# Unread matrix products in the doubling, ahead of the sparse attention's transposes and of block 1's output product

## The chip, the cores and the metric

The kernel runs on one core of a Trainium2 chip. Five engines work beside each other and wait for one another through semaphores: TensorE (PE in the profile; its weight loads are PEld), VectorE (DVE), ScalarE (ACT), GpSimd (POOL) and SyncE (SP), which issues most transfers. [...] The metric is the time of one execution on the device in microseconds, the median of several runs.

## The reference

The reference puts two blocks of two layers each behind one another, on 256 tokens of width 1024. A layer of block 1 mixes three attention branches and ends with one output product. A layer of block 2 runs three mixers side by side (gated linear attention, RWKV-7, sparse attention), an output product, a norm and a feed-forward part. What the change stands next to is this:

```python
# block 1, end of a layer
merged = jnp.sum(gates * up, axis=2)
return x + jnp.einsum('bsd,de->bse', merged, w_out)

# block 2, RWKV-7: one step per token
def step(state, inp):
    r_t, w_t, k_t, v_t, a_t, b_t = inp
    sa = jnp.einsum('bhvk,bhk->bhv', state, a_t)
    state = (state * w_t[:, :, None, :] + sa[..., None] * b_t[:, :, None, :]
             + v_t[..., None] * k_t[:, :, None, :])
    return state, jnp.einsum('bhvk,bhk->bhv', state, r_t)

# block 2, sparse attention: selected keys, and a window
pr = jax.nn.softmax(s, axis=-1)
return jnp.einsum('bghqnk,bgqnkd->bqghd', pr.astype(vg.dtype), vg)
```

With 256 tokens the selection and the window both hold all keys up to the query, so the kernel computes two causal attentions.

## The kernel before

**Tiling.** The tokens are two tiles of 128, the heads 64 wide. Weights come as a stream of pieces of 128x1024 through SyncE's queue (`unit`, L294); ScalarE rounds each to fp32r (`whi`, L295) and VectorE takes the rest (`wlo`, L272). Three products (L329 to L331 in `mm3`) then give an almost exact fp32 result; plain fp32 products go by L327.

**The doubling** (`rwkv`, L792). The steps of a 128-token tile are written as a triangular system. Its inverse is built by doubling in five levels, `q` from 1 to 5, for both tiles and four heads at once. A level has two rounds of sixteen 64x64 products: the first (L931) multiplies `M` with `Pm` into a pair of PSUM banks, and VectorE multiplies the pair with a mask (`r_X`, called at L933); the second (L951) multiplies `Qm` with `X`, VectorE adds the old `Pm` (`r_P`, L953), TensorE transposes it (L407) and ScalarE copies it out (`r_Q`, L908). The last level's second round (L959, L960) has another form. Each round uses columns 0 to 255 of its two banks. The bank pair comes from a pool that holds one pair, so the steps of a level follow each other. In the gaps the program has other work of the layer: products of the gated linear attention (L1120), of the compressed attention (L1216, L1247, L1289, L1309) and of RWKV itself (L888, L942).

**The sparse attention** (`nsa_direct`, L1258, through `causal_attn`, L534, and `softmax_pv`, L513). For each token tile and each of two key sets it goes in groups of up to four heads: scores (L547), the causal mask as one bf16 product of constants (`negb`, `causb`, L550), maximum (L518), scaling (L520), exponentials (L524), four transposes into one bank (`transposed`, L403, L407), a copy (L528) and the products with the values (L531). That is two groups for the first tile and four for the second, twelve in a layer. Scores, transposes and the attention's output take their banks from a pool of three, which other helpers share (`ps`, L248).

**Block 1's output product** (`out_proj`, L376, called by `block1_layer`, L652). Its left operand is split by ScalarE (`mh`, L400) and VectorE (`ml`, L275), and its weights come in four units; both must be there before the first products.

**Order.** The program is written as a list, and a planner orders it when the kernel is built: each instruction gets a running number, and among those that are ready in the planner's model the lowest goes first. `with self.sec(name)` (L204) shifts the numbers of a section by an entry of the table `AHEAD` (L1532). Each engine then runs its list in order. A PSUM buffer of a pool is taken when its first writer is placed and comes free behind its last reader.

Of the kernel before, what the change touches and what calls it, by code (L numbers as in the profile page):

```python
# [151 lines left out]
class Kern:  # L152
# [95 lines left out]
    def ps(self, *shape):  # L248
        return self.bank(self.pa, *shape)
# [123 lines left out]
        for p in range(2):  # L373
            done(p, ps[p])

    def out_proj(self, tags, parts, ps, ws, first=0, n=None, skew=0):  # L376


        n = n or len(tags)

        def go(i, tt, cg):
            h, lo = parts[i]
            sl = slice(128 * tt, 128 * tt + 128)
            for kk in range(2):
                self.mm3(ps[tt][cg], (h[:, kk, sl], lo[:, kk, sl]), w[i](1024 * kk + 512 * cg, 512),
                         first + i + kk == 0, first + i == n - 1 and kk == 1)
        w = [ws[i] if i in ws else self.unit(t) for i, t in enumerate(tags)]
        m = len(tags) - skew
        for i, tt, cg in ([(i, tt, cg) for i in range(m) for tt in range(2) for cg in range(2)] +
                          [(i, tt, cg) for tt in range(2) for cg in range(2) for i in range(m, len(tags))]):  # L390
            go(i, tt, cg)
# [8 lines left out]
            nc.scalar.activation(h, src, AF.Copy, scale=scale)  # L400
            self.stt(l, src, scale, h.bitcast(F32), ALU.mult, ALU.subtract)

    def transposed(self, ps, srcs):  # L403

        pt = ps(4, 128)
        for j, s in enumerate(srcs):
            self.nc.tensor.transpose(pt[:, j], s, self.ident)  # L407
        return pt[:, :len(srcs)]
# [14 lines left out]
    def rms(self, xs, g, xT, ps=None, out=None):  # L423

        nc = self.nc
        for tt in range(2):
            x = xs[tt]
            ss = self.sm.tile([128, 2], F32, name="ss")
            o = out[tt] if out is not None else self.u("xn", D)
            for cg in range(2):  # L430
                cs = slice(512 * cg, 512 * cg + 512)
                if ps is not None:
                    self.tt_(x[:, cs], ps[tt][cg], x[:, cs], ALU.add)
                nc.scalar.activation(xT.space(cg)[:, :, 128 * tt:128 * tt + 128], x[:, cs].rearrange("p (c s) -> p c s", c=4), AF.Square,
                                     accum_out=ss[:, cg:cg + 1])
            ms = self.sm.tile([128, 2], F32, name="ms")
            self.tt_(ms[:, 0:1], ss[:, 0:1], ss[:, 1:2], ALU.add)
            nc.vector.tensor_scalar(ms[:, 1:2], ms[:, 0:1], 1.0 / D, 1e-6, op0=ALU.mult, op1=ALU.add)
            rs = self.sm.tile([128, 1], F32, name="rs")
            nc.gpsimd.tensor_tensor(out=rs, in0=ms[:, 1:2], in1=self.mhalf[:, 0:1], op=ALU.pow)  # L440
            for cg in range(2):
                cs = slice(512 * cg, 512 * cg + 512)
                self.stt(o[:, cs], x[:, cs], rs, g[cg], ALU.mult, ALU.mult)
                if xT is not None:
                    xT.put(o[:, cs], cg, tt)

    def deep_norm(self, x, ps, w, b, xT=None, out=None, pool=None):

        nc = self.nc
        for tt in range(2):  # L450
            t = [self.u("dn") for cg in range(2)]
            st = self.sm.tile([128, 2, 6], F32, name="dn_s")
            for cg in range(2):
                cs = slice(512 * cg, 512 * cg + 512)
                self.stt(t[cg], x[tt][:, cs], ALPHA, ps[tt][cg], ALU.mult, ALU.add)
                nc.vector.bn_stats(out=st[:, cg], in_=t[cg])
            mv = self.sm.tile([128, 4], F32, name="dn_m")
            nc.vector.bn_aggr(out=mv[:, 0:2], in_=st.rearrange("p a b -> p (a b)"))
            nc.vector.tensor_scalar(mv[:, 2:3], mv[:, 1:2], 1e-5, None, op0=ALU.add)
            nc.gpsimd.tensor_tensor(out=mv[:, 3:4], in0=mv[:, 2:3], in1=self.mhalf[:, 0:1], op=ALU.pow)  # L460
            for cg in range(2):
                self.stt(t[cg], t[cg], mv[:, 0:1], w[cg], ALU.subtract, ALU.mult)
            for cg in range(2):
                cs = slice(512 * cg, 512 * cg + 512)
                self.stt(x[tt][:, cs], t[cg], mv[:, 3:4], b[cg], ALU.mult, ALU.add)
                if xT is not None:
                    xT.put(x[tt][:, cs], cg, tt, ps=pool)
                if out is not None:
                    nc.sync.dma_start(out[0, 128 * tt:128 * tt + 128, cs], x[tt][:, cs])

# [39 lines left out]
        self.nc.scalar.activation(t, ps, AF.Tanh, scale=0.5)  # L510
        self.stt(dst, t, 1.0, ps, ALU.add, ALU.mult)

    def softmax_pv(self, sv, heads, nk, scale, vt, o, ocol, den, first, last):  # L513

        nc = self.nc
        nh = len(heads)
# [6 lines left out]
        for i, h in enumerate(heads):  # L523
            nc.scalar.activation(p3[:, i], sv[:, i], AF.Exp, bias=nb[:, i:i + 1], scale=scale,  # L524
                                 accum_out=den[:, h:h + 1])
        pt = self.transposed(self.ps, [p[:, 128 * j:128 * j + 128] for j in range(nh * nk)])
        ps = self.u("ptsb", 4, 128)
        nc.scalar.copy(ps, pt)  # L528
        for i, h in enumerate(heads):
# [1 line left out]
                nc.tensor.matmul(o[:, ocol(h)], ps[:, i * nk + k, :], vt(k, h),  # L531
                                 start=first and i == 0 and k == 0, stop=last and i == nh - 1 and k == nk - 1)

    def causal_attn(self, qT, kT, v, tt, o, den, mask=None):  # L534

        nc = self.nc
        nk = tt + 1
# [5 lines left out]
        for gi, heads in enumerate(groups):  # L543
# [8 lines left out]
            else:  # L552
                nc.tensor.matmul(s3, self.negb, mask[:, None, :].to_broadcast([128, hs, 128 * nk]), start=False, stop=True)
            self.softmax_pv(s3, heads, nk, 0.125, v, o, lambda h: slice(64 * h, 64 * h + 64), den,
                            gi == 0, gi == len(groups) - 1)

    def gate_out(self, o, den, g2, nh, ysT, tt):

# [93 lines left out]
    def block1_layer(self, l, hT, mem):  # L652
# [70 lines left out]
        with self.sec("hw"):  # L723
            held = {1: self.unit(f"wo{l}.1", tag="vg")}
        with self.sec("wo"):
            self.out_proj([f"wo{l}.{u}" for u in range(4)], parts, ps, held, skew=3)
        return ps


# [62 lines left out]
    def rwkv(self, l, R, wa, g0, tl, P, hp, rows, out):  # L792
# [84 lines left out]
        half = (lo, up)  # L877
        tiles = [(tt, c) for tt in both for c in range(2)]
        quads = [(n, j, b) for n in range(4) for j in both for b in both]
        pair = lambda: self.pair(self.pr)[:, :, 0:256].rearrange("p a (n k) -> p a n k", n=4)  # L880
        eye = cst["eye64"]

        def products(tt, nm, st, pool):
# [11 lines left out]

        Pm = self.u("r_P", 4, 2, 64)
        nc.gpsimd.tensor_copy(Pm, eye[:, None, None].to_broadcast([128, 4, 2, 64]))
        ps = pair()
        for n, j, b in quads:
            tt, c = tiles[n]  # L900
            mm(ps[half[b], j, n], ar4[tt][half[j], 0, c, half[b]], Bt[half[j], c, 128 * tt + 64 * b:128 * tt + 64 * b + 64],
# [23 lines left out]
        rest = list(both)  # L925
        rhs, yv = [], self.c3("r_yv")
        for q in range(1, 6):
            ps = pair()
            for n, j, b in quads:
                tt, c = tiles[n]  # L930
                mm(ps[half[j], b, n], M[tt]["MB", j][half[b], c, 0, half[b]], Pm[half[b], n, j], start=n == 0, stop=n == 3)  # L931
            X = self.u("r_X", 2, 4, 64)
            self.tt_(X, ps, self.minv[:, 64 * q - 64:64 * q][:, None, None].to_broadcast([128, 2, 4, 64]), ALU.mult)  # L933
            if rest:
# [10 lines left out]
                nc.scalar.copy(yv[:, t0], ps[:, 1].rearrange("p h d -> p (h d)"))  # L945
                if t0:
                    nc.gpsimd.tensor_copy(rhs[t0][:, :, 64:128], TM[t0][:, 1].rearrange("p (h d) -> p h d", d=64))
            ps = pair()
            if q < 5:
                for n, j, b in quads:  # L950
                    mm(ps[half[b], j, n], Qm[half[j], n, b], X[half[j], b, n], start=n == 0, stop=n == 3)  # L951
                Pn = self.u("r_P", 4, 2, 64)
                self.tt_(Pn.rearrange("p n j k -> p j n k"), ps, Pm.rearrange("p n j k -> p j n k"), ALU.add)  # L953
                Pm = Pn
# [303 lines left out]
    def nsa_direct(self, qT, kT, vt, gc, out):  # L1258
# [3 lines left out]
        for tt in range(2):  # L1262
# [4 lines left out]
            for i, n in enumerate("sw"):  # L1267
                o = self.ps()
                self.causal_attn(qT[tt], lambda pr, h, m: kT[n][pr, :m], lambda k, h: vt[n][k][:, 64 * (h % 2):64 * (h % 2) + 64],
                                 tt, o, den[:, i])  # L1270
                nc.vector.reciprocal(cf[:, i], den[:, i])
                self.tt_(cf[:, i], cf[:, i], gate[:, 1 + i], ALU.mult)
                t = acc if i == 0 else self.u("n_t")
                self.tt_(h3(t), h3(o), cf[:, i, :, None].to_broadcast([128, 8, 64]), ALU.mult)
                if i:
                    self.tt_(acc, acc, t, ALU.add)
# [145 lines left out]
    def run(self, out, stop=None):  # L1422
        nc = self.nc
        with self.block(BUFS1):
            mem = self.mem_kv(0, nc.sync)
            self.load_first()
            kv = mem()
# [38 lines left out]
class Feat:  # L1466
# [5 lines left out]
        self.h = [kern.u(name + "h", 4, 256, dt=F32R) for _ in range(n // 4)]  # L1472
        self.l = [kern.u(name + "l", 4, 256, dt=F32R) for _ in range(n // 4)]

    def put(self, src, g, tt, scale=1.0, ps=None):

        pt = self.k.transposed(ps or self.k.ps, [src[:, 128 * j:128 * j + 128] for j in range(4)])
        sl = slice(128 * tt, 128 * tt + 128)
        self.k.split(pt, self.h[g][:, :, sl], self.l[g][:, :, sl], scale)

# [26 lines left out]
class Both(Feat):  # L1507
# [3 lines left out]
        super().__init__(kern, n, name)  # L1511
        self.w = Whole(kern, n, name)

    def put(self, src, g, tt, scale=1.0, ps=None):
        pt = self.k.transposed(ps or self.k.ps, [src[:, 128 * j:128 * j + 128] for j in range(4)])
        sl = slice(128 * tt, 128 * tt + 128)
        self.k.split(pt, self.h[g][:, :, sl], self.l[g][:, :, sl], scale)
        self.k.nc.scalar.copy(self.w.f[g][:, :, sl], pt)
# [11 lines left out]
         "r_g2 r_y r_RW r_yn r_ynx r_ynq dsh f_h f_l f_t oh ol",  # L1530
}.items() for n in names.split()}
AHEAD = dict(x=-107, x2=172, m01=267, n12=1422, h1=368, n3=-94, rwkv=38, cmp=242, w=-330, cpd=-15, h2=179, ww=-425, out=-24, gla=-582, ofg=488, ln2=-168, atta=-78, gin=-106, tok=36, imask=-432, rx1=-342, attb=-197, rxf=517, w1=15, feat=5, nsa=-131, ofn=-323, rx0=25, hw=499, ofr=-116, hd=-14, rin=10, prep=298, wo=-87, ln1=298)  # L1532
ALPHA = float((2 * DEPTH) ** 0.25)
SMALL = ["x", "mem", "norm_g", "mem_norm_g", "final_g", "ln1_w_2", "ln1_b_2", "ln2_w_2", "ln2_b_2"]
P_MU, P_W0, P_A0, P_V0, P_KK, P_KA, P_BA, P_RK, P_POSK, P_POSV, P_W2K, P_W2V, P_WA, P_G2, P_TAIL = (
# [69 lines left out]
```

## Time and profile before

| | |
|---|---|
| time, median of 3 runs | 1604.45 us (1598.08 to 1605.7) |
| the profiled execution's own time | 1608.67 us |
| its span, first to last instruction | 1606.6 us |
| mean granted clock of TensorE | 0.958 |
| busy: PE, PEld | 1543.5 us (96%), 1319.0 us (82%) |
| busy: DVE, ACT, POOL | 918.8 us (57%), 721.0 us (45%), 42.8 us (3%) |

Times of instructions are counted from the start of the span. A busy PE is not PE at its peak: products overlap, and their ends are modelled, so the distance from one start to the next tells what one costs. [...] Idle time stands before the instruction that ended it, with what it waited for.

### The profile page before, as it was taken

To read this page: it belongs to the slowest core of one execution; us is meant where nothing else is said; L and a number is where in the kernel's file an instruction comes from. 1 tells how busy PE (TensorE), PEld (TensorE's weight loads), DVE (VectorE), ACT (ScalarE), POOL (GpSimd) and SP (SyncE) were. 2 spreads that over 40 slices of the span, in tenths; PEclk is the share of its full clock that TensorE was granted. 3 is DMA by queue.
4 is the path that set the end of the run, shared out by engine and by line. 5 is a ranking of instruction groups with operands and counts; after the bars stand their busy time and mean duration, and the time that the engine had idled before them with its cause. 6 is when DMAs were issued, how large, how long until landed. Compare 5 with 4: busy or idle time off the path is not lost.

```text
span 1606.6 us, 25450 instructions
## 1 busy us (share of the span) xinstructions
PE 1543.5 (96%) x10196; PEld 1319.0 (82%) x10196; DVE 918.8 (57%) x1511; ACT 721.0 (45%) x1302; POOL 42.8 (3%) x82
## 2 busy tenths in 40 slices
PE   7999999999999999999999989999999999999997
PEld 6877899979878899868767769998797577789986
DVE  5566455565585455564445675556745455765554
ACT  5555544445454544454632234444355422344441
POOL 0000000000000000000001010000000000100000
PEclk9999999999999999999986899999999976999999
DMA  8643435455524345556301245557445111265560
GB/s 272 226 129 132 157 106 168 161 172 192 187 99 158 106 131 183 160 187 197 116 27 53 71 136 179 185 168 238 134 157 167 40 54 41 66 197 194 187 210 27
DMA packets 72982, 231.66 MB, mean 144 GB/s; under 512 B 8736, under 2 KB 11552, under 8 KB 72864
## 3 DMA queue, kind: packets, MB, share of 16 engines
q1 hardware_dynamic: 67248, 219.74, 41.5%
q10 hardware_dynamic: 5616, 10.30, 2.0%
q8 instruction: 80, 1.31, 0.3%
q14 instruction: 38, 0.31, 0.1%
HBM read 228.96 MB, written 1.05 MB: 143 GB/s over the span
## 4 chain that ended last, share of the span: by engine, by line
PE 44%; DVE 4%; ACT 3%; DMA 3%; issue 2%; POOL 0%; ACTq 0%; DVEq 0%
PE ps L329 9%; PE ps L331 9%; PE ps L330 9%; PE ps L327 3%; PE ps L407 3%; DMA raw<-in_stream_dram 2%; PE ps L1120 2%; PE ps L547 1%; PE ps L531 1%; DVE wlo L272 1%; PE ps L942 1%; ACT whi L295 1%; PE ps L888 1%; PE ps L931 1%; DVE xlo L272 0%
## 5 line engine op out<-in xcount | busy, mean ns | idle before, releaser
L272 DVE TENSOR_TENSOR wlo<-raw,whi 128x1024 fp32r<-128x1024 f32 (+2 forms) x364 | 427.8, 1184 | 324.3 <-ACT whi L295 321.3
L295 ACT CAST whi<-raw 128x1024 fp32r<-128x1024 f32 (+2 forms) x364 | 367.3, 1018 | 385.5 <-PE ps L330 165.4
L329 PE MATMUL ps<-xTh,whi 128*128 128x256 f32 x720 | 205.4, 285 | 5.2 <-ACT whi L295 4.0
L331 PE MATMUL ps<-xTh,wlo 128*128 128x256 f32 x720 | 205.1, 285 | 1.5 <-DVE wlo L272 1.5
L330 PE MATMUL ps<-xTl,whi 128*128 128x256 f32 x720 | 204.7, 284 | 0.0
L329 PEld LDWEIGHTS ps<-xTh,whi 128*128 128x128 f32 x720 | 138.5, 192 | 6.8 <-ACT whi L295 4.4
L331 PEld LDWEIGHTS ps<-xTh,wlo 128*128 128x128 f32 x720 | 138.6, 193 | 2.1 <-DVE wlo L272 2.1
L330 PEld LDWEIGHTS ps<-xTl,whi 128*128 128x128 f32 x720 | 138.5, 192 | 0.8
L330 PE MATMUL ps<-wlo,hTh 128*128 128x512 f32 (+2 forms) x352 | 135.8, 386 | 0.8 <-DVE wlo L272 0.8
L329 PE MATMUL ps<-whi,hTh 128*128 128x512 f32 (+2 forms) x352 | 134.9, 385 | 0.3 <-ACT wi L667 0.3
L331 PE MATMUL ps<-whi,hTl 128*128 128x512 f32 (+2 forms) x352 | 132.9, 378 | 0.0
L329 PE MATMUL ps<-hTh,whi 128*128 128x256 f32 x448 | 128.9, 288 | 0.0
L330 PE MATMUL ps<-hTl,whi 128*128 128x256 f32 x448 | 128.5, 287 | 0.0
L331 PE MATMUL ps<-hTh,wlo 128*128 128x256 f32 x448 | 127.6, 285 | 0.0
L524 ACT ACTIVATE pexp<-ps,nb 128x256 f32<-128x256 f32 (+1 forms) x144 | 60.0, 425 | 65.6 <-DVE nb L520 60.3
L329 PEld LDWEIGHTS ps<-hTh,whi 128*128 128x128 f32 x448 | 85.8, 192 | 0.8
L330 PEld LDWEIGHTS ps<-hTl,whi 128*128 128x128 f32 x448 | 85.7, 191 | 0.7
L331 PEld LDWEIGHTS ps<-hTh,wlo 128*128 128x128 f32 x448 | 85.7, 191 | 0.5
L329 PEld LDWEIGHTS ps<-whi,hTh 128*128 128x128 f32 x352 | 66.2, 188 | 13.9 <-issue 2.0
L330 PEld LDWEIGHTS ps<-wlo,hTh 128*128 128x128 f32 x352 | 66.3, 188 | 10.7 <-DVE wlo L272 1.2
L331 PEld LDWEIGHTS ps<-whi,hTl 128*128 128x128 f32 x352 | 66.2, 188 | 10.6
L518 DVE TENSOR_REDUCE mx<-ps 128x2 f32<-128x512 f32 (+1 forms) x56 | 38.6, 689 | 61.5 <-PE ps L550 39.9
(463 smaller groups left out, 3031.8 us busy)
## 6 DMA issues: line engine op xcount, KB each, us to landing
raw<-in_stream_dram SPq DMA_DIRECT2D x346, 512.0 KB, 4.1
raw<-in_stream_dram SPq DMA_DIRECT2D x56, 256.0 KB, 3.1
whi<-in_stream_dram SPq DMA_DIRECT2D x11, 512.0 KB, 4.2
wlo<-in_stream_dram SPq DMA_DIRECT2D x11, 512.0 KB, 6.4
row<-in_ln_w_dram ACTq DMA_DIRECT2D x8, 256.0 KB, 3.3
row<-in_ln_b_dram ACTq DMA_DIRECT2D x8, 256.0 KB, 4.1
raw<-in_stream_dram SPq DMA_DIRECT2D x4, 480.0 KB, 4.4
raw<-in_stream_dram SPq DMA_DIRECT2D x4, 420.0 KB, 4.5
```

What stands on the lines that cost most here:

```text
L272: self.nc.vector.tensor_tensor(out=out, in0=a, in1=b, op=op)
L295: nc.scalar.copy(hi[:, :b - a], raw)
L327: mm(out, a, b, start=start, stop=stop)
L329: mm(out, a[0], b[0], start=start, stop=False)
L330: mm(out, a[0], b[1], start=False, stop=False)
L331: mm(out, a[1], b[0], start=False, stop=stop)
L407: self.nc.tensor.transpose(pt[:, j], s, self.ident)
L518: nc.vector.tensor_reduce(out=mx[:, :nh], in_=sv, axis=AX.X, op=ALU.max)
L524: nc.scalar.activation(p3[:, i], sv[:, i], AF.Exp, bias=nb[:, i:i + 1], scale=scale, accum_out=den[:, h:h + 1])
L531: nc.tensor.matmul(o[:, ocol(h)], ps[:, i * nk + k, :], vt(k, h), start=first and i == 0 and k == 0, stop=last and i == nh - 1 and k == nk ...
L547: nc.tensor.matmul(s3[:, i], qT[pr, h // 2], kT(pr, h, 128 * nk), start=i == 0, stop=False)
L1120: mm(ps[j][:, tt, c], a, e, start=tt + c == 0, stop=c == 1 and (tt == 1 or m == 128))
```

## The change

Matrix products whose results nothing reads are added in three places. Their operands are the two constants of the causal mask, bf16, 128x128 weights. A new table `KEEP` says how many go where; the entries that are zero add nothing.

- `lev=2`: behind each round of sixteen of the doubling, but not behind the last level's second round, two products of 256 columns, one into the unused columns 256 to 511 of each of the round's two banks. That is 18 per layer.
- `nsa=1`: in each of the twelve groups of the sparse attention, one product of 512 columns into the bank that the transposes then fill. The attentions of block 1 call the same helper without it.
- `wo=3`: ahead of block 1's output product, three products of 512 columns into the first two banks of its sums, which the output product then overwrites.

```diff
-    def out_proj(self, tags, parts, ps, ws, first=0, n=None, skew=0):
+    def out_proj(self, tags, parts, ps, ws, first=0, n=None, skew=0, keep=None):
...
         m = len(tags) - skew
+        if first == 0 and keep:
+            self.busy(keep, ps[0][0], ps[0][1])
         for i, tt, cg in ([(i, tt, cg) for i in range(m) for tt in range(2) for cg in range(2)] +
...
+    def busy(self, where, *banks):
+
+        for n in range(KEEP[where]):
+            o = banks[n % len(banks)]
+            n = int(np.prod(o.shape[1:])) // 128
+            o = o if len(o.shape) == 3 else o.rearrange("p (a t) -> p a t", t=128)
+            self.nc.tensor.matmul(o, self.negb, self.causb[:, None, :].to_broadcast([128, n, 128]), start=True, stop=True)
+
-    def transposed(self, ps, srcs):
+    def transposed(self, ps, srcs, where=None):
 
         pt = ps(4, 128)
+        if where:
+            self.busy(where, pt)
         for j, s in enumerate(srcs):
...
-        pt = self.transposed(self.ps, [p[:, 128 * j:128 * j + 128] for j in range(nh * nk)])
+        pt = self.transposed(self.ps, [p[:, 128 * j:128 * j + 128] for j in range(nh * nk)], keep)
...
-            self.out_proj([f"wo{l}.{u}" for u in range(4)], parts, ps, held, skew=3)
+            self.out_proj([f"wo{l}.{u}" for u in range(4)], parts, ps, held, skew=3, keep="wo")
...
-        pair = lambda: self.pair(self.pr)[:, :, 0:256].rearrange("p a (n k) -> p a n k", n=4)
+
+        def pair():
+
+            t = self.pair(self.pr)
+            return t[:, :, 0:256].rearrange("p a (n k) -> p a n k", n=4), [t[:, a, 256:512] for a in both]
...
         for q in range(1, 6):
-            ps = pair()
+            ps, idle = pair()
             for n, j, b in quads:
                 tt, c = tiles[n]
                 mm(ps[half[j], b, n], M[tt]["MB", j][half[b], c, 0, half[b]], Pm[half[b], n, j], start=n == 0, stop=n == 3)
+            self.busy("lev", *idle)
...
             if q < 5:
                 for n, j, b in quads:
                     mm(ps[half[b], j, n], Qm[half[j], n, b], X[half[j], b, n], start=n == 0, stop=n == 3)
+                self.busy("lev", *idle)
...
-                                 tt, o, den[:, i])
+                                 tt, o, den[:, i], keep="nsa")
...
+KEEP = dict(lev=2, nsa=1, gla0=0, gla1=0, wo=3, rms00=0, rms01=0, rms10=0, rms11=0, ln100=0, ln101=0, ln110=0, ln111=0, ln200=0, ln201=0, ln210=0, ln211=0, start=0)
```

The table `AHEAD` is unchanged. The other hunks hand `where` and `keep` through the helpers for places whose entry is zero.

## Rows read from the trace of the kernel before

**Rows 1.** The page: span, granted clock in 40 slices, chain by engine.
```profile
span 1606.6 us, 25450 instructions
...
PEclk9999999999999999999986899999999976999999
...
PE 44%; DVE 4%; ACT 3%; DMA 3%; issue 2%; POOL 0%; ACTq 0%; DVEq 0%
```

**Rows 2.** Stretches: length, busy PE, PEld, DVE, ACT, POOL, clock, DMA.
```profile
668.42:675.25 6.83, 6.55 (x15) 4.68 (x16) 6.83 (x10) 1.31 (x2) 0.00 (x0) 0.50 0.39 109
804.95:811.78 6.83, 6.83 (x18) 3.98 (x17) 0.86 (x2) 1.02 (x4) 0.00 (x0) 0.50 0.01 2
828.85:832.26 3.41, 3.12 (x10) 1.59 (x8) 3.28 (x5) 1.67 (x8) 2.31 (x3) 0.50 0.00 0
856.15:883.46 27.31, 27.31 (x159) 22.65 (x158) 9.89 (x31) 5.79 (x19) 2.68 (x11) 0.50 0.06 20
893.70:903.94 10.24, 9.85 (x144) 8.61 (x146) 7.36 (x17) 2.45 (x6) 0.00 (x0) 0.50 0.02 4
1255.51:1258.93 3.42, 3.42 (x8) 1.70 (x8) 0.86 (x2) 1.02 (x4) 0.00 (x0) 0.50 0.00 0
...
1303.30:1332.30 29.00, 28.48 (x172) 22.12 (x168) 13.47 (x34) 7.67 (x20) 0.40 (x1) 0.50 0.14 49
1332.30:1354.50 22.20, 21.14 (x309) 18.03 (x310) 14.65 (x31) 4.74 (x9) 0.00 (x0) 0.50 0.10 33
```

**Rows 3.** Order of time, PE, line 531: start us, us, instruction.
```profile
805.27 1.97 PE L531 MATMUL ps<-n_vs,ptsb 128*128 128x64 f32 x8
...
813.67 1.10 PE L531 MATMUL ps<-n_vs,ptsb 128*128 128x64 f32 x8
```

**Rows 4.** Order of time, line 931: levels three and four.
```profile
883.67 0.69 PE L931 MATMUL ps<-r_P,r_M 64*64 64x64 f32 x32
...
889.46 0.69 PE L931 MATMUL ps<-r_P,r_M 64*64 64x64 f32 x32
...
1332.27 1.13 PE L931 MATMUL ps<-r_P,r_M 64*64 64x64 f32 x32
...
1339.49 1.14 PE L931 MATMUL ps<-r_P,r_M 64*64 64x64 f32 x32 [0.68 <-ACT r_Q L908]
```

**Rows 5.** Order of time: the mask's product and its successor.
```profile
814.61 0.27 PE L550 MATMUL ps<-causb,negb 128*128 128x256 bf16 x1
...
814.72 1.88 PE L327 MATMUL ps<-whi,xTf 128*128 128x512 f32 x4
```

**Rows 6.** Order of time, line 951: first level's second sixteen.
```profile
854.03 0.69 PE L951 MATMUL ps<-r_X,r_Q 64*64 64x64 f32 x30
...
1306.89 0.69 PE L951 MATMUL ps<-r_X,r_Q 64*64 64x64 f32 x10
```

**Rows 7.** Stretches of 2 us around two falls, layer 0.
```profile
854.00:856.00 2.00, 1.95 (x41) 1.69 (x40) 1.99 (x5) 0.49 (x3) 0.60 (x2) 1.00 0.48 154
856.00:858.00 2.00, 2.00 (x12) 2.00 (x12) 1.27 (x3) 0.12 (x1) 0.91 (x5) 0.54 0.67 216
...
890.00:892.00 2.00, 0.34 (x23) 0.20 (x17) 2.00 (x5) 0.63 (x1) 0.00 (x0) 1.00 0.62 209
```

**Rows 8.** Groups by line, 757 to 842 us: busy us, mean ns, idle before.
```profile
L407 PE MATMUL ps<-c_ident,pexp 128*128 128x128 f32 x48 | 10.6, 305 | 2.7 <-ACT pexp L524 2.6
```

**Rows 9.** Order of time, PE, line 407: the longest such wait.
```profile
803.26 0.89 PE L407 MATMUL ps<-c_ident,pexp 128*128 128x128 f32 x4 [1.44 <-ACT pexp L524]
```

**Rows 10.** Order of time, PE, line 330: block 1's second output product.
```profile
668.61 0.79 PE L330 MATMUL ps<-wlo,mh 128*128 128x512 f32 x1 [1.36 <-DVE wlo L272]
```

**Rows 11.** Stretches: the same place of both output products.
```profile
329.06:334.85 5.79, 5.25 (x22) 4.01 (x23) 5.79 (x9) 1.12 (x2) 0.00 (x0) 1.00 0.57 182
668.61:674.40 5.79, 5.70 (x13) 4.02 (x14) 5.79 (x9) 1.12 (x2) 0.00 (x0) 0.50 0.40 119
```

More of the change, by code (lines that the diff above doesn't have):

```diff
@@ L444, in rms @@
                 if xT is not None:
-                    xT.put(o[:, cs], cg, tt)
+                    xT.put(o[:, cs], cg, tt, where=None if ps is None else f"rms{tt}{cg}")
     def deep_norm(self, x, ps, w, b, xT=None, out=None, pool=None):
@@ L466, in deep_norm @@
                 if xT is not None:
-                    xT.put(x[tt][:, cs], cg, tt, ps=pool)
+                    xT.put(x[tt][:, cs], cg, tt, ps=pool, where=f"{'ln1' if pool else 'ln2'}{tt}{cg}")
                 if out is not None:
@@ L511, in silu2, with softmax_pv @@
         self.stt(dst, t, 1.0, ps, ALU.add, ALU.mult)
-    def softmax_pv(self, sv, heads, nk, scale, vt, o, ocol, den, first, last):
+    def softmax_pv(self, sv, heads, nk, scale, vt, o, ocol, den, first, last, keep=None):
         nc = self.nc
@@ L532, in softmax_pv, with causal_attn @@
                                  start=first and i == 0 and k == 0, stop=last and i == nh - 1 and k == nk - 1)
-    def causal_attn(self, qT, kT, v, tt, o, den, mask=None):
+    def causal_attn(self, qT, kT, v, tt, o, den, mask=None, keep=None):
         nc = self.nc
@@ L554, in causal_attn @@
             self.softmax_pv(s3, heads, nk, 0.125, v, o, lambda h: slice(64 * h, 64 * h + 64), den,
-                            gi == 0, gi == len(groups) - 1)
+                            gi == 0, gi == len(groups) - 1, keep)
     def gate_out(self, o, den, g2, nh, ysT, tt):
@@ L927, in rwkv @@
         for q in range(1, 6):
-            ps = pair()
+            ps, idle = pair()
             for n, j, b in quads:
@@ L947, in rwkv @@
                     nc.gpsimd.tensor_copy(rhs[t0][:, :, 64:128], TM[t0][:, 1].rearrange("p (h d) -> p h d", d=64))
-            ps = pair()
+            ps, idle = pair()
             if q < 5:
@@ L1424, in run @@
         with self.block(BUFS1):
+            if KEEP["start"]:
+                t = self.u("g")
+                nc.gpsimd.memset(t, 1.0)
+                o = self.ps()
+                for _ in range(KEEP["start"]):
+                    nc.tensor.matmul(o, t[:, 0:64].bitcast(BF16), t[:, 0:256].bitcast(BF16), start=True, stop=True)
             mem = self.mem_kv(0, nc.sync)
@@ L1473, in __init__, with put @@
         self.l = [kern.u(name + "l", 4, 256, dt=F32R) for _ in range(n // 4)]
-    def put(self, src, g, tt, scale=1.0, ps=None):
-        pt = self.k.transposed(ps or self.k.ps, [src[:, 128 * j:128 * j + 128] for j in range(4)])
+    def put(self, src, g, tt, scale=1.0, ps=None, where=None):
+        pt = self.k.transposed(ps or self.k.ps, [src[:, 128 * j:128 * j + 128] for j in range(4)], where)
         sl = slice(128 * tt, 128 * tt + 128)
@@ L1512, in __init__, with put @@
         self.w = Whole(kern, n, name)
-    def put(self, src, g, tt, scale=1.0, ps=None):
-        pt = self.k.transposed(ps or self.k.ps, [src[:, 128 * j:128 * j + 128] for j in range(4)])
+    def put(self, src, g, tt, scale=1.0, ps=None, where=None):
+        pt = self.k.transposed(ps or self.k.ps, [src[:, 128 * j:128 * j + 128] for j in range(4)], where)
         sl = slice(128 * tt, 128 * tt + 128)
```

## The prediction

> **What bounds the kernel now.** I read the page first, then the clock by stretches of time, then the order of instructions in the three places that the change touches. [...] What a half-level microsecond is worth is read from the same work at both levels: eight products on n_vs take 1.97 us at half level and 1.10 us at full [rows 3], a saving of 0.44 where TensorE alone is the limit. Late in the doubling it is less: from the third level's products to the fourth's it takes 7.22 us in layer 1 (half level) and 5.79 us in layer 0 (full), a saving of 0.20, since VectorE and ScalarE then come into the chain [rows 4].
>
> **What the change adds, part by part.** It removes and moves nothing and adds no DMA; per layer it adds 18 products of 256 columns behind the doubling's sixteens, 12 of 512 ahead of the sparse attention's transposes, and 3 of 512 ahead of block 1's output product, 66 in all. Their operands are constants loaded at the start. The price of one is read from the causal mask's product, the same bf16 operands: 256 columns start at 814.61 us and the next product at 814.72, so 0.11 us of TensorE's queue at full level [rows 5]; I take 0.22 us for 512 columns, and twice each at half level.
>
> *Doubling.* Cost: 36 x 0.11 = 4.0 us, with nothing hidden, since TensorE is the chain there; at half level 36 x 0.22 = 7.9 us, the other end. The pair writes the unused columns of the two banks that VectorE reads next (r_X, r_P), so VectorE may wait for it; that wait is the same 0.22 us per pair, already counted, and behind VectorE wait the next sixteen. Gain: no row shows an unread product in this stretch, so the part of the half level that it wins back is bounded by none and all. All is 27.31 x 0.44 = 12.0 and 29.00 x 0.44 = 12.8 for the parts bound by TensorE, and 22.20 x 0.20 = 4.4 and 10.24 x 0.20 = 2.0 for the late parts: 31.2 us. What I take goes by where the products fall. In layer 0 the first level's second sixteen end at 854.72 us, so a pair would run 1.4 us ahead of the fall at 856.15 [rows 2, 6]; and the fall at 893.70 follows a slice in which TensorE was busy for 0.34 of 2.00 us, which the next pairs sit in [rows 7]. There I take all, 14.0 us. In layer 1 part of the same sixteen still runs at 1306.89, behind the fall at 1303.30, so the pair comes too late for that fall [rows 2, 6] and can only bring the clock back sooner: I take half of 17.2, 8.6 us. Together 22.6 us.
>
> *Sparse attention.* Cost: 24 x 0.22 = 5.3 us if nothing hides them, nothing if all sit in waits. The transposes of layer 0 waited 2.7 us in twelve groups [rows 8], and 1.44 us of that in one of them [rows 9]; a group without a wait pays in full, so I take 4.0, nearer the upper end. The product needs only a free bank, the transposes need the exponentials: it will run ahead of them, in that wait. Behind it on TensorE's queue stand the transposes, and ScalarE's copy of them waits for those. Gain: between none and 13.66 x 0.44 = 6.0 us; the worst wait (1.44 us, at 803.26) stands just ahead of the fall at 804.95, the other two falls follow no such row that I read, so I take half, 3.0.
>
> *Output product.* Cost: 6 x 0.22 = 1.3 us if bare; the wait of 1.36 us for the split weights in layer 1 covers three of them [rows 10], so I take 0. In layer 0 the clock does not fall there, so nothing is to be won. In layer 1 TensorE runs 13 instructions at half level in the 5.79 us after that wait, where layer 0 ran 22 at full level in 5.79 us of the same place [rows 11]; nine of 0.23 us are 2.1 us, which I take whole because the fall comes inside that wait. None is the other end.
>
> *Order.* The planner places instructions by a running number that shifted sections count from, so 66 new ones can reorder the neighbours of such sections. No row prices that; I allow 4 us either way, half the distance between the fastest and slowest run shown (7.6 us).
>
> Sum: -22.6 + 4.0 - 3.0 + 4.0 - 2.1 = -19.7 us. The profiled execution took 1608.67 us (its span 1606.6 and 2.1 around it), so 1589.0 by its own time; it stands 4.2 us above the median of the runs, and against that median the forecast is 1585 us.
>
> [...] The slices around the first fall show TensorE busy for 1.95 and 2.00 of 2.00 us while the clock drops [rows 7]: the engine hardly idles, its work is thin. [...]
>
> **The rivals.** *1, all is won:* every stretch of the table [rows 2] runs at full level. For it: thin work holds most of them. Then -31.2 + 4.0 - 6.0 + 4.0 - 2.1 = -31.3, 1573 us. *2, only layer 0 is held:* in layer 1 the pairs come behind the fall and change nothing, and run at half level: -14.0 + 18 x 0.11 + 18 x 0.22 - 3.0 + 4.0 - 2.1 = -9.2, 1595 us. [...] *4, slower:* the sparse attention's bank. Today the transposes take their bank when the exponentials are done; the product takes it as soon as one is free, out of three, and TensorE's queue runs in order, so whatever else needs a bank there (the next scores, the other mixer's products) waits behind it. A group that loses as much as the longest wait [rows 9] pays 1.44 us; 24 of them pay 34.6, against the forecast's -19.7: +14.9, 1619 us. It is slower than the bound below from about 19 groups on (19 x 1.44 = 27.4, against 19.7 + 8.0). Against it: the next scores stand behind the transposes in the trace anyway.
>
> **How the numbers follow.** A measurement of this kernel can tell about 0.5% from no change, 8.0 us: faster is below 1596.4, slower above 1612.5. Chances: the forecast 0.45 (its own range 1576 to 1596: the halves I took give about 6 either way, the order 4), rival 1 0.12, rival 2 0.18, rival 3 0.13, rival 4 0.12. Faster: 0.43 + 0.12 + 0.10 = 0.65; same: 0.02 + 0.08 + 0.11 = 0.21; slower: 0.02 + 0.12 = 0.14. The range reaches from just under rival 1 to rival 3 with its order on top, 1571 to 1611, and leaves out rival 4 and the ends.
>
> **What would show it.** Right: in the table of stretches the clock of layer 0's doubling stays at its full level and layer 1's half-level stretch shrinks to about 25 us; the level from third to fourth products in layer 1 takes near 5.8 us; the mean granted clock rises from 0.958 to about 0.98; the products show 0.11 and 0.22 us from start to start. Wrong: half-level stretches as long as before (rival 3), layer 1's unchanged (rival 2), or longer waits of TensorE ahead of scores and transposes in the sparse attention (rival 4).

## The result, and the profile after

The changed kernel takes 1604.53 us (median of 20 runs, 1599.50 to 1615.91) against 1600.67 us for the kernel before in the same comparison: a ratio of 1.0081, with an interval of 1.0056 to 1.0106. It is slower by under 1%, where 1585 us and faster was forecast. Ratios come from comparisons that leave disturbed runs out; the means of spans and clocks further down are over all runs. The plain means of the 20 times of each, 1605.5 and 1599.9 us, give 1.0035 (1.0011 to 1.0059): both intervals lie above 1, and the size of the loss is less sure than its sign. The profiled execution took 1614.99 us; its span is 1613.1 us, its mean granted clock 0.963, the lowest of its 20 runs (mean 0.972). Full level is a granted clock of 1.00 and half level one of 0.50; a value between is a stretch with both, as 0.54 in 856.00:858.00 of [rows 7], which is at 1.00 up to 856.15 us and at 0.50 from there.

The page of the changed kernel, its span, its granted clock in 40 slices and the chain by engine, which answer to [rows 1]:

```profile
span 1613.1 us, 25584 instructions
...
PEclk9999999999999999999995699999999997999999
...
PE 44%; DVE 5%; ACT 3%; DMA 3%; issue 2%; POOL 1%; ACTq 0%; DVEq 0%
```

The dip of layer 0 is deeper than before, the one of layer 1 shallower. The view by stretches shows how long they are (columns as in [rows 2]):

```profile
670.70:674.10 3.40, 3.26 (x7) 2.14 (x8) 3.40 (x6) 0.38 (x2) 0.00 (x0) 0.50 0.63 176
762.80:769.60 6.80, 6.80 (x25) 5.48 (x25) 1.70 (x6) 1.81 (x10) 0.00 (x0) 0.50 0.18 75
851.60:882.30 30.70, 29.50 (x175) 21.82 (x172) 14.88 (x42) 7.13 (x20) 4.82 (x12) 0.50 0.04 12
882.30:913.00 30.70, 30.70 (x339) 24.99 (x343) 18.89 (x36) 7.03 (x13) 0.40 (x1) 0.50 0.21 68
1268.00:1271.40 3.40, 3.40 (x12) 2.43 (x12) 0.86 (x2) 0.69 (x3) 0.00 (x0) 0.50 0.00 0
1302.10:1305.50 3.40, 2.65 (x26) 1.17 (x26) 3.31 (x5) 1.28 (x2) 0.00 (x0) 0.50 0.00 0
1343.10:1360.10 17.00, 16.82 (x222) 13.34 (x222) 10.76 (x25) 3.77 (x8) 0.00 (x0) 0.50 0.02 8
```

Layer 0's doubling has one fall of 61 us where before had 27.31 and 10.24; layer 1's has 17 instead of 51 [rows 2]. As this execution has the lowest clock of 20, a usual run falls for less: 2 x 0.037 x 1613.1 = 119 us at half level here, 90 in the mean of the 20. The output product's went from 6.83 to 3.4 us. The next view is the order of time on TensorE around layer 0's fall, from the first level's first sixteen (L948 is L931 of before, L412 the unread products, L1235 the products on `n_X`, L969 the second sixteen):

```profile
842.99 0.45 PE L948 MATMUL ps<-r_P,r_M 64*64 64x64 f32 x12
844.56 0.64 PE L1235 MATMUL ps<-whi,n_X 128*32 128x256 f32 x8 [1.12 <-issue]
...
848.41 0.33 PE L948 MATMUL ps<-r_P,r_M 64*64 64x64 f32 x4
848.67 0.39 PE L412 MATMUL ps<-causb,negb 128*128 128x256 bf16 x2
848.90 0.95 PE L1112 MATMUL ps<-c_ones,g_E 128*128 128x2 f32 x8
...
851.02 1.57 PE L905 MATMUL ps<-r_AR,r_K 64*128 64x256 f32 x6 [0.68 <-ACT r_tm L936]
853.73 1.97 PE L1266 MATMUL ps<-P,n_hv 128*128 128x64 f32 x8 [1.14 <-POOL n_hv L1262]
855.49 1.86 PE L1308 MATMUL ps<-n_kc,n_qT 128*128 128x30 f32 x8
857.28 1.22 PE L905 MATMUL ps<-r_AR,r_K 64*128 64x256 f32 x2
858.43 0.81 PE L969 MATMUL ps<-r_X,r_Q 64*64 64x64 f32 x20
```

A pair of unread products takes 0.23 us here, 848.67 to 848.90, as priced. It stands behind the first sixteen, runs 2.9 us ahead of the fall at 851.6 and does not prevent it. What follows it is not what followed before: the `n_X` products, which filled the wait for the second sixteen, have run by 846.4, and what is left up to 858.4 is mostly thin, products of 2 to 64 columns with a few transposes and products of 256 columns between, and two waits of 0.68 and 1.14 us. The planner has put half of the `n_X` products ahead of the doubling in each layer, where before had all inside.

Another line that changed is a wait behind the doubling: TensorE waits for `yr`, RWKV's output. First the kernel before, then the changed one (the table of waits: us in total, times, longest):

```profile
PE ps L407 <- DVE yr L272: 3.0, 2, 1.5
```

```profile
PE ps L420 <- DVE yr L272: 5.8, 2, 3.8
```

Ahead of block 1's second output product the three unread products do not stand in the wait that the prediction put them in: they run ahead of the first product, and the wait for the split weights behind it is 1.37 us, where it was 1.36 [rows 10].

```profile
667.12 0.82 PE L412 MATMUL ps<-causb,negb 128*128 128x512 bf16 x3
668.71 0.49 PE L329 MATMUL ps<-whi,mh 128*128 128x512 f32 x1 [0.77 <-ACT mh L402]
670.58 0.74 PE L330 MATMUL ps<-wlo,mh 128*128 128x512 f32 x1 [1.37 <-DVE wlo L272]
```

Of the lines that answer to the rest of the rows, the level from third to fourth products [rows 4] now takes 6.64 us in layer 1 (it straddles the fall at 1343.1) and 9.42 in layer 0, which now runs it at half level:

```profile
889.45 1.13 PE L948 MATMUL ps<-r_P,r_M 64*64 64x64 f32 x32
...
898.87 1.13 PE L948 MATMUL ps<-r_P,r_M 64*64 64x64 f32 x32
...
1338.83 0.69 PE L948 MATMUL ps<-r_P,r_M 64*64 64x64 f32 x32
...
1345.47 0.81 PE L948 MATMUL ps<-r_P,r_M 64*64 64x64 f32 x20
```

### The profile page after: what moved, and what is told of

It is laid out like the page before. It is cut to its first block, busy times and chain, and to the rows that moved or that the text cites. A ratio compares the mean times of both kernels' runs of the same rounds, so it can differ in the third digit from the quotient of the medians.

```text
span 1613.1 us, 25584 instructions
## 1 busy us (share of the span) xinstructions
PE 1545.4 (96%) x10262; PEld 1317.2 (82%) x10262; DVE 916.9 (57%) x1511; ACT 722.5 (45%) x1302; POOL 44.6 (3%) x82
## 4 chain that ended last, share of the span: by engine, by line
PE 44%; DVE 5%; ACT 3%; DMA 3%; issue 2%; POOL 1%; ACTq 0%; DVEq 0%
PE ps L329 9%; PE ps L331 9%; PE ps L330 9%; PE ps L327 3%; PE ps L420 2%; DMA raw<-in_stream_dram 2%; PE ps L1139 2%; PE ps L560 2%; PE ps L544 1%; DVE wlo L272 1%; ACT whi L295 1%; PE ps L905 1%; PE ps L412 1%; PE ps L960 1%; DVE xlo L272 1%
```

## A way to read all runs at once

One execution shows one set of falls, but nearly every run lists its span and its mean clock. From these, the time at half level in a run is 2 x (1 - clock) x span. Over the 282 runs that list both (114 of them of the kernel before, taken beside the experiments) one straight line fits each kernel: **span = span at full level + 0.396 x time at half level**, with the slope common to all, and runs scatter 1.8 us about it. So a kernel has two numbers: what it would take if the clock never fell, and how long it falls on average.

| kernel (runs) | mean span | mean us at half level | span at full level |
|---|---|---|---|
| before (114) | 1594.3 | 101 | 1554.1 |
| changed (20) | 1603.6 | 90 | 1568.1 |
| products_alone (12) | 1583.1 | 60 | 1559.3 |
| products_alone_x4 (12) | 1588.9 | 53 | 1568.1 |
| order_alone (6) | 1603.5 | 100 | 1563.9 |
| order_bare (12) | 1599.2 | 98 | 1560.4 |
| doubling_only (12) | 1589.6 | 70 | 1561.7 |
| sparse_only (12) | 1606.6 | 116 | 1560.5 |
| sparse_kept (12) | 1589.2 | 82 | 1556.8 |
| output_only (12) | 1596.8 | 107 | 1554.5 |
| dense_ahead (12) | 1581.6 | 72 | 1553.0 |
| dense_inside (12) | 1594.2 | 71 | 1566.1 |
| ahead_doubling (10) | 1580.4 | 54 | 1558.9 |
| both_kept (12) | 1584.7 | 55 | 1563.0 |
| ahead_both (12) | 1588.8 | 68 | 1562.1 |

The standard error of a mean is 1.5 to 8 us for the time at half level and under 1 us for the span at full level. The changed kernel is 14.0 us dearer at full level and gets 12 us of half level back, worth 4.7: together the 9.3 us by which its mean span is longer. The 20 runs of before in its own comparison list no clock; against their mean time it is 5.6 us longer.

## The experiments

The first question was whether the products do the harm or the planner's new order. The planner's running numbers are not it: when the kernel is built with the numbers advanced by one for each product, but without the products, every engine's list comes out as before. It is the products themselves, which take time and banks in the planner's model, that change it. So some kernels below get their products after the planner is through, in the order of the kernel before ("kept order"), by this addition (its main lines), which puts them behind each sixteen and lets VectorE's wait hold for the last of them:

```diff
+    for i in list(block.instructions):
+        done.append(i)
+        if i.name in last and last[i.name][1] == 16:
...
+            for k in range(2):
+                o = bass.AP(tensor=last[i.name][0], offset=512 * (k % 2) + 256, ap=[[1024, 128], [1, 256]])
...
+                nc.tensor.matmul(o.rearrange("p (a t) -> p a t", t=128), const["negb"], rhs, start=True, stop=True)
...
+            done += every[start:]
```

**products_alone**: this addition to the kernel before.

> The kernel before with its instruction order kept as it is; the 36 products of 256 columns are put behind the sixteens of the doubling after the planner is through. Theory A (the order): the products hold no clock, the half-level stretches of the two doublings stay as before within one of the short ones (layer 0 some 38 us in two, layer 1 some 51 us) and the time rises by the price of the products alone, 36 x 0.11 to 0.19 = 4 to 7 us, a ratio of 1.0025 to 1.0045. Theory B (the products): the stretches become those of the changed kernel, some 61 us in layer 0 and 17 us in layer 1, at least one of the two moving by over 15 us.

Measured: 0.9927 (0.9883 to 0.9972), faster. At full level it costs 5.1 us, inside the price expected, and the time at half level goes from 101 to 60 us, worth 16.4. Its profiled execution has a clock of 0.969, below the mean of its runs (0.981), and still shows shorter falls than before (two stretches of layer 0's doubling, at full and at half level, then the fall of layer 1's):

```profile
840.40:864.70 24.30, 23.07 (x270) 16.81 (x269) 14.88 (x33) 10.21 (x28) 3.12 (x9) 1.00 0.27 88
864.70:878.35 13.65, 13.65 (x79) 11.37 (x79) 5.96 (x18) 1.84 (x5) 1.48 (x5) 0.50 0.00 1
1305.00:1332.30 27.30, 26.78 (x167) 20.39 (x160) 11.86 (x32) 6.64 (x18) 0.40 (x1) 0.50 0.07 26
```

Neither theory had this: in this order the products do hold the clock, and the harm is not in them.

**products_alone_x4**: the same with `range(8)`.

> The kernel before in its own order with eight products of 256 columns behind each sixteen instead of two, 144 in all. If unread products can hold the clock at all and two were too few: layer 0's stretch and layer 1's go (up to 31 us by the forecast's bounds) for a price of at most 144 x 0.11 = 15.8 us, so some 15 us faster, ratio 0.99. If they cannot: the stretches stay and the price is 144 x 0.11 to 0.19 = 16 to 27 us, ratio 1.010 to 1.017.

Measured: 0.9993 (0.9950 to 1.0035). The price is 13.9 us at full level, the time at half level 53 us. In its profile both doublings run at full level from end to end:

```profile
836.30:890.00 53.70, 51.41 (x713) 40.51 (x712) 37.06 (x82) 18.84 (x46) 4.57 (x14) 1.00 0.24 80
1280.60:1333.00 52.40, 49.58 (x640) 38.34 (x640) 37.98 (x84) 18.50 (x44) 2.90 (x7) 1.00 0.20 72
```

So unread products can hold the clock there, but six more products per sixteen cost 8.8 us more and take away some 8 us of half level, which is no more than the scatter of the two means: two are better than eight.

**order_alone**: the changed kernel; each unread product is cut to one column after planning.

```diff
+            o = bass.AP(tensor=o.tensor, offset=o.offset, ap=[o.ap[0], [1, 1]])
+            rhs = bass.AP(tensor=rhs.tensor, offset=0, ap=[rhs.ap[0], [1, 1]])
```

> The changed kernel with its instruction order and its waits kept, and each of the 66 unread products cut to one column. Theory A (the order): the stretches at half level stay those of the changed kernel (some 61 us in layer 0's doubling, 17 us in layer 1's) and the time falls by the price of the products, at most 36 x 0.19 + 24 x 0.22 + 6 x 0.22 = 13 us and rather half of it, so a ratio of 1.000 to 1.005 to the kernel before. Theory B (the products): the stretches go back to those of before, 38 and 51 us. Rival C (the sparse attention's bank, taken early): the loss ahead of the doubling, some 3 us over both layers, stays, since the waits stay.

Measured: 1.0109 (1.0050 to 1.0167). The loss is there without the products' columns; theory A's ratio was too low. The profile has 34 us at half level in layer 0's doubling, nearer to B, and 17 in layer 1's, as A had it; one execution does not decide that, and 100 us on average is as much as before. At full level it costs 9.7 us more than before, of which 3.5 are gone in the next kernel, which has no unread products at all; so 66 products of one column are not free.

**order_bare**: the same order, products and their weight loads taken out, their waits left in.

```diff
+        if i.debug and i.debug.lineno == 413 and i.debug.bass_funcname == "Kern.busy":
...
+                waits += i.sync_info.on_wait
...
+            continue
```

> The changed kernel's instruction order with all 66 unread products and their weight loads taken out; their waits go to the next product. From the runs so far a span is its time at full level plus 0.41 us for each us at half level; before stands at 1552.6 us plus 100 us at half level, the changed kernel at 1566.9 plus 90, the order with one-column products at 1562.5 plus 100. If the new order costs time by itself, some 6 us of those 10 stay when the products are gone altogether: 1558 plus 100, ratio 1.003 to 1.006. If the 10 us are the 66 instructions themselves, it stands at 1553 plus 100: ratio 0.999 to 1.002.

Measured: 0.9993 (0.9949 to 1.0037); 1560.4 us at full level plus 98 at half level. The ratio falls in the second branch, the mean span (4.9 us longer) and the fit in the first: 6.2 us at full level belong to the order (with the waits that the products left in it) alone. In its profile layer 0's doubling falls where the changed kernel's does, between the first level's two sixteens, without any unread product (columns as in [rows 2]):

```profile
845.20:882.70 37.50, 35.95 (x213) 27.95 (x212) 18.59 (x50) 10.49 (x29) 6.68 (x14) 0.50 0.11 37
```

A part of the 6.2 us can be pointed at, the wait behind the doubling, which is 5.7 us here as in the changed kernel:

```profile
PE ps L421 <- DVE yr L273: 5.7, 2, 3.8
```

In the changed kernel 92 of the trace's records of the gated linear attention's `g_E` products lie inside layer 1's doubling where before had 72; that less is then left to cover this wait is likely, but no run tests it. The longer wait shows in every planned order with products for the doubling or the sparse attention (5.3 to 7.7 us) and in none of the kept ones (2.9 or 3.0 us; the kernel before has 3.0). The other 3.5 us are spread over several stages and were not pinned down.

**doubling_only** (`nsa=0, wo=0` in `KEEP`), **sparse_only** (`lev=0, wo=0`) and **output_only** (`lev=0, nsa=0`): one part each, ordered by the planner.

> The change with the products of the doubling alone (none in the sparse attention, none ahead of the output product), ordered by the planner. Theory A (the order): its doubling stands in a third order, and its stretches at half level are neither those of before nor those of the changed kernel: no size can be told, but the two layers need not move alike. Theory B (the products): the doubling behaves as in the changed kernel, layer 0 some 10 us longer than before, layer 1 some 4 us shorter, ratio 1.003 to 1.006.

Measured: 0.9995 (0.9945 to 1.0044). Against products_alone, the same 36 products in the kept order, the planner's order costs 2.4 us more at full level; the 10 us more that it leaves at half level are no more than the scatter of the two means. Layer 0 did not behave as in the changed kernel, whose doubling of layer 0 falls for 61 us: the profiled execution here has a clock of 0.982 and a span of 1583.0 us, so 57 us at half level in all, and neither of B's numbers came.

> The change with the sparse attention's products alone. Theory D (dense work moved ahead): with these products the planner puts 16 of the 32 products of 512 columns on n_X (the compressed attention's first layer) ahead of each layer's doubling, where the kernel before has all 32 inside. So the doubling of layer 1 starts some 8 us later and runs emptier: 8 to 11 us more at full level, up to 24 x 0.22 = 5.3 us for the products, and no less time at half level than before (some 100 us): ratio 1.006 to 1.012. Rival (the doubling's own products do the harm): ratio 0.998 to 1.003.

Measured: 1.0086 (1.0052 to 1.0119), as theory D had it, with 6.4 us at full level and 116 us at half level. This part alone is at least as slow as the whole change. One statement in the expectation is off: the 32 products on `n_X` of a layer have 256 columns each and leave two records apiece in the trace; eight records take 0.43 us, so that the half which is moved is 1.7 us of TensorE.

> The change with the three products ahead of block 1's output product alone; the n_X products stay inside the doubling. Theory D: nothing of the 8 us ahead of layer 1's doubling appears; block 1's half-level stretch shrinks from 6.83 to 3.41 us, worth 1.4 us; ratio 0.996 to 1.001. Rival (any re-ordering costs, wherever it comes from, since the planner's table was fitted to the old order): ratio above 1.003.

Measured: 1.0028 (0.9986 to 1.0071): no difference at full level (0.3 us), and 107 us at half level are not told from 101. The stretch in block 1 shrank to 3.4 us as expected, but order_bare, sparse_kept and dense_ahead, which have no product there, show 3.4 us in their profiles too, so the shrinking is no sign of the products.

**dense_ahead** and **dense_inside** test whether the move of the `n_X` products is what costs. One number of the planner's table changes, in the kernel before to 140, in the changed kernel to -211; other neighbours move with them.

```diff
 AHEAD = dict(
...
-nsa=-131
+nsa=140
...
```

> The kernel before without any unread product; one number of the planner's table is changed (the sparse attention's entry from -131 to 140), which puts all 32 products on n_X ahead of the doubling in both layers. Theory D: the doubling starts later by some 10 us or more in both layers and falls to half level for as long as before or longer: 5 to 16 us slower, ratio 1.004 to 1.010. Rival C (the sparse attention's bank, taken early by the unread product, is what costs): there is no such product here, so ratio 0.998 to 1.002.

Measured: 0.9936 (0.9908 to 0.9965), **faster**. Theory D falls in this form: with all `n_X` products ahead of the doubling in both layers (below, layer 0's up to the doubling's start) the kernel costs nothing more at full level and spends 72 us at half level, without one unread product.

```profile
L1216 PE MATMUL ps<-raw,n_X 128*32 128x256 f32 x24 | 1.9, 382 | 1.0 <-DVE n_X L272 1.0
L1216 PE MATMUL ps<-whi,n_X 128*32 128x256 f32 x24 | 1.9, 382 | 0.5 <-issue 0.5
L1216 PE MATMUL ps<-wlo,n_X 128*32 128x256 f32 x16 | 1.3, 379 | 0.0
```

> The changed kernel with all its 66 products; one number of the planner's table is changed (the sparse attention's entry from -131 to -211), which puts all 32 products on n_X back inside the doubling. Theory D: the 8 us ahead of layer 1's doubling go, the time at half level falls to that of the doubling's products alone (60 to 70 us a run), and the ratio is 0.994 to 1.001. Rival C (the bank): the loss stays, ratio 1.005 to 1.010.

Measured: 1.0014 (0.9976 to 1.0052). All 66 products, another order, and no loss is left to be seen: the time at half level is 71 us instead of 90, the price at full level stays (11.9 us). Rival C, the bank, would have kept the loss; the sparse attention's waits speak against it too, since the transposes' wait of [rows 8], 2.7 us, is 0.3 us in the changed kernel (the same 48 transposes, groups by line):

```profile
L420 PE MATMUL ps<-c_ident,pexp 128*128 128x128 f32 x48 | 9.3, 282 | 0.3 <-ACT pexp L537 0.3
```

**sparse_kept**: the 24 products in the kept order, behind the transposes' wait instead of ahead of it.

```diff
...
+            o = bass.AP(tensor=o.tensor, offset=0, ap=[o.ap[0], [1, 512]])
...
+                new = copy.replace(new, sync_info=told(on_wait=i.sync_info.on_wait, on_update=[]))
```

> The kernel before in its own order with the sparse attention's 24 products of 512 columns put right ahead of the transposes after the planner is through, behind the wait for the exponentials (so no bank is taken early and no order changes). If the products are harmless but for their price: 24 x 0.22 = 5.3 us at most, the time at half level as before (some 100 us), ratio 1.001 to 1.0035. If they harm the clock by themselves: some 115 us at half level as in the run with the sparse attention's products alone, ratio 1.006 to 1.010.

Measured: 0.9939 (0.9897 to 0.9982). Price 2.6 us at full level, and 82 us at half level where sparse_only had 116. The same 24 products lose 12 us of mean span in the planner's order and win 5 in the old one; by the plain means of all runs that win is a ratio of 0.9965, give or take 0.004.

**both_kept**: the two sets of products in the kept order, and **ahead_doubling** and **ahead_both**: the doubling's, and both, in the order of dense_ahead.

> The kernel before in its own order with the doubling's 36 products and the sparse attention's 24, both put in after the planner is through: the change but for its six products at the output product, without the new order. If prices and gains add up: full-level span 1553.9 + 5.3 + 2.8 = 1562 us, time at half level 102 - 42 - 21 = 39 us, so 1562 + 0.4 x 39 = 1577.6 us of span against 1594.6 for the kernel before, ratio 0.987 to 0.991. If both cure the same falls: some 60 us at half level, 1586 us, ratio 0.993 to 0.997. If the loss is in the products after all: ratio 1.00 or above.

Measured: 0.9941 (0.9898 to 0.9984). The prices come to 8.8 us together (5.1 and 2.6 alone). The gains don't seem to add up: 55 us are left at half level, little less than the doubling's products leave alone, though the scatter of these means, some 13 us, leaves the 41 us of a full sum possible. In its profile layer 0's doubling runs at full level throughout, layer 1's falls for 27 us:

```profile
836.40:884.00 47.60, 44.30 (x608) 33.85 (x610) 35.50 (x81) 18.19 (x43) 4.70 (x14) 1.00 0.27 90
...
1295.00:1322.30 27.30, 26.78 (x163) 20.44 (x160) 11.85 (x32) 6.56 (x18) 0.40 (x1) 0.50 0.08 28
```

> The two edits that were faster, together: all products on n_X ahead of the doubling (the planner's entry for the sparse attention at 140), and the 36 products of 256 columns behind the sixteens put in after the planner is through. If what they save at half level adds up (72 us left by the one, 40 taken away by the other): 1552 + 6 + 0.41 x 30 = 1570 us of span, ratio 0.983 to 0.988. If they cure the same falls: 1558 + 0.41 x 60 to 72 = 1583 to 1588 us, ratio 0.992 to 0.996.

Measured: 0.9909 (0.9873 to 0.9945), the best ratio of the study: 54 us at half level, and at full level 4.7 us more than before (5.9 more than dense_ahead), between the sum and the overlap. Against dense_ahead (0.9936) the intervals overlap.

> The same two sets of products put into the order in which all products on n_X stand ahead of the doubling. Full level 1552.9 + 5.9 + 2.8 = 1561.6 us; the order with the doubling's products alone had 54 us left at half level, of which the sparse attention's products take 0 to 20: span 1575 to 1583 us, ratio 0.988 to 0.993.

Measured: 0.9992 (0.9962 to 1.0021), slower than expected: the sparse attention's products cost 3.2 us at full level and leave 68 us at half level where ahead_doubling left 54. Here they were put in behind the planner and moved nothing, and the kernel still got slower, with intervals that do not touch. So these products can do harm without a new order too, and by these runs what they do depends on the order that they are put into; why, no run shows.

## Why the prediction was wrong

**The step that failed** is the one named *Order*: "No row prices that; I allow 4 us either way", with nothing in the sum. It was the largest term. With it goes the prediction's "It removes and moves nothing": the planner moved much. The runs give the time at half level for the two orders with and without products (both_kept has 60 of the 66, and its sparse attention's products stand behind the wait for the exponentials instead of ahead of it):

| | without | with | won |
|---|---|---|---|
| order of before | 101 | 55 | 46 us, worth 18.5 |
| the planner's new order | 98 | 90 | 8 us, worth 3.3 |

The 46 us are good to some 6 us and the 8 to some 7, so that the second can't be told from none. In the order that the trace of before showed, nearly the same products make the kernel faster. The new order costs 6.2 us at full level and takes some 15 us of what the products would win there; the products' own price, 7.8 us at full level in the new order, is what was forecast in sum (4.0 + 4.0). The forecast read the neighbours of each product from a trace in which the planner had not yet seen it. The cause given for a reorder was wrong too: not the numbers, but the time and the bank that a product takes in the planner's model. Why the products win so little in the new order stays open in part. Shown is that it is the order (dense_inside, with the same products in another one, has 71), and where layer 0 falls: in the thin stretch between the first level's two sixteens, in the profile of order_bare too. That half of the `n_X` products are missing there was the theory, and dense_ahead, where all are missing, did not fall longer (72 us at half level, before 101).

**Bound.** In the stretches of [rows 2] TensorE is busy 91% of the time or more (least in 828.85:832.26, 3.12 of 3.41 us) at a clock of 0.50, and that it bounds them stands. The one at 668.42 lies in block 1's output product, those at 804.95, 828.85 and 1255.51 in the sparse attention, 13.66 us together, the others in the doubling. A half-level microsecond was taken as worth 0.44 or 0.20 [rows 3, 4]; over all runs it is worth 0.396.

**Doubling.** The price of 0.11 and 0.22 us a product held (0.23 us for a pair at full level where 0.22 was taken), and 5.1 us for the 36 lies between the two ends given. The gain, 22.6, is 16.4 in the kept order. That "a pair would run 1.4 us ahead of the fall at 856.15" was no reason to take all: in the changed kernel the pair behind the first sixteen ran 2.9 us ahead, and the clock fell; the pair that was meant, behind the second sixteen, came only after that fall. Layer 1's number came out near the forecast (17 us in the changed kernel, 27 in products_alone, 25 forecast), in the changed kernel by luck: with the products' columns or the products gone, order_alone shows 17 and order_bare 10 us there, in one profile each.

**Size of the gains.** The bounds came from one execution with a clock of 0.958: 2 x 0.042 x 1606.6 = 135 us at half level. The mean of before is 101, so a quarter of what was to be won was not there in a usual run. The correction by 4.2 us to the median was too small for that, because it moved the start and not the gain.

**Sparse attention.** The price was 2.6 us (4.0 taken), the gain in the kept order 7.8, give or take 3 (3.0 taken); in the planner's order this part loses 12. **Output product.** Price and gain are not told from nothing. That the wait of 1.36 us covers the three products was a wrong reading: they run ahead of that wait, and it is as long as before.

**Rivals.** Rival 4 had the right sign, the right place (the sparse attention) and the wrong mechanism: TensorE's wait for the exponentials fell from 5.5 to 2.4 us, and the unread products themselves waited 0.7 us in all. The wait ahead of the `n_X` products, for which the profile names no releaser, did grow, from 0.5 to 2.8 us, but it is 3.6 us in order_bare, without the products. Rival 3, half-level stretches as long as before and 1609 us in the forecast's range, falls with products_alone and products_alone_x4, which have 60 and 53 us at half level where before has 101; why the clock should fall as before was not shown. The stretches of [rows 7] have hardly any idle time ahead of the first fall (1.95 of 2.00 us busy), but 0.34 of 2.00 us busy ahead of the second, so in this trace idle time stands ahead of some of the falls and not of all. No run here parts the two kinds.

## What to carry to other kernels

When a planner orders the program, an added instruction is first of all another order: compare the two lists before pricing the instruction, and test it in the old order. Read the clock from many runs (span against mean clock) before taking the falls of one profile as the kernel's own; it separates what an edit costs from what it does to the clock. An entry of the planner's table can be worth as much as added work: one number won 0.6% here, without any product.

## What was not expected of the hardware

The scatter of this kernel is its clock: the mean granted clock of before goes from 0.954 to 0.984 over 114 runs of one program, and with it the span, so that 1.8 us of scatter is left once the clock is taken out. These runs show the scatter, but not where it comes from. The falls in the midst of this kernel cost 101 us x 0.396 = 40 us, 2.5% of its mean span of 1594.3 us.
